# Three more w_down pairs with a second row unit by seven products, and two small kinds of buffers moved to the 2 KB pool

## The chip, the cores and the metric

One core of a Trainium2 chip (trn2) runs the whole kernel. The metric is the time of one execution on the device in microseconds (us), the median of several runs.

## The reference

Two layers of a decoder trunk on 256 tokens with 2048 features, all in fp32. What matters here is the second half of a layer, the SwiGLU block, whose last product is the one that the change touches:

```
for l in range(DEPTH):
    ...                                   # norm, projections, attention, spatial gating, merge
    x = x + merged @ w_out[l]
    h2 = rms_norm(x, ffn_norm[l])
    x = x + (jax.nn.silu(h2 @ w_gate[l]) * (h2 @ w_up[l])) @ w_down[l]
```

w_gate and w_up are 2048 x 5632, w_down is 5632 x 2048.

## The kernel before

**One product.** Every weight is read once, in halves of 256 rows x 512 columns (512 KB, tile `raw`). ScalarE (ACT) rounds a half to fp32r, tile `whi` (L261); VectorE (DVE) makes what is left over, `wlo = raw - whi` (L262). The tokens lie transposed on TensorE's other side, split the same way into `uh` and `ul`. A product of one 128-token tile with a half is six matmuls of 128x128 by 128x512: for each of two blocks of 128 rows, whi by uh, wlo by uh, whi by ul (L361, L362). An ordinary entry of the list does this for both token tiles, so twelve matmuls.

**Pairs and row units.** Column chunks of 512 are taken in pairs, a and b. A row unit is two halves (512 rows) of both chunks; with two token tiles this is a 2 x 2 by 2 x 2 product of blocks, which takes eight products of six matmuls in the plain way (entries G for a, U for b) or seven by Strassen's scheme in Winograd's form (entries P1, P5, P2, P6, P7, P4, P3, one product each). The scheme wants four differences of raw halves, made in place on DVE (L246), and so seven splits by L261 and L262 in place of four; and on the token side four sums with a split of their own: `flat`, `sums`, `sh` and `sl`, made once for a unit of tokens (L520 and L506 for unit 0, L539, L546, L551 and L552 in `summed` for unit 1). Six products are the head of a pair (P3 comes later): their entries are interleaved with the last entries of the pair ahead (L198 to L216).

Every pair has one row unit by seven products. A pair marked `two` has a second one. The raw halves of that second unit lie in the pool `big` (31 slots of 4 KB a partition), those of the first in four single buffers `k11`, `k12`, `k21`, `k22` of the pool `wraw`. When P5 is done, one accumulator is evicted to a tile `kept` (L384) and another copied (L385); P6 and P7 fold theirs into `kept` (L387); the two results start the accumulators of chunk b (L390, `acc<-kept`).

**Rounds.** The hidden width is worked in rounds of 4, 4 and 3 chunks (`ROUNDS`). A round makes its chunks of w_gate and w_up (key `ffn`, one pair of a gate and an up chunk for each f), and then multiplies by its rows of w_down: two pairs of output chunks (key `hid`, j = 0 and j = 2). The first two rounds of a layer are the middle rounds of this text: their result is a part of the residual sum. ACT evicts each accumulator to a tile `part` (L963), and a DMA on GpSimd's queue (POOL) adds it to the residual in DRAM, `held_x` (L964). The last round adds to the residual on DVE.

**What sets the order.** TensorE (PE) runs in the order in which the program is written, entry by entry. `Stream.next` asks for weights seven entries ahead, splits four ahead (`W_SPLIT`; four buffers each of whi and wlo), and makes the differences six ahead (`W_SUM`). Work on tokens is put into slots by `after` and `tick`; for the token sums of unit 1, `W_HID` is 15 slots after the ffn pair of chunk 1. The order on the other engines is set by the framework's scheduler, and each engine runs its list strictly in order. A tile of a pool takes a buffer that is free; where none is, its first writer waits for the last reader of an old one. The pool `tmp` has four buffers of 2 KB a partition.

Of the kernel before, what the change touches and what calls it, by code (L numbers as in the profile page):

```python
# [11 lines left out]
ALU = mybir.AluOpType  # L12
# [27 lines left out]
WINO_END = 9, 10, 12, 13, 14, 15  # L40
W_SPLIT = 4
X_FETCH = 2
HID_TWO = (1, 2, 2), (0, 0, 0), (1, 0, 0), (0, 0, 2), (1, 0, 2), (1, 1, 2),
W_HID = 15
FFN_TWO = (1, 0), (1, 1), (1, 2), (2, 0), (2, 1), (2, 2), (1, 3), (0, 2)
W_TWO = 17
# [17 lines left out]
def hybrid_trunk(ctx: ExitStack, tc: tile.TileContext, x, mix_norm, w_in, q_norm, k_norm, sinks,  # L64
# [299 lines left out]
    def step():  # L364
        e = entries[stream.at]
        p, tag = e["plan"], e["tag"]
        units = units_at[p.key]
        w = stream.next()
        if tag in "XGU":
            ps = banks(p, "b" if tag == "U" else "a")  # L370
            todo = [(ps[t], block(units, e["h"], t)) for t in range(NT)]
        else:
            which, t, form = {"P1": ("a", 1, (0, 0)), "P2": ("a", 0, (1, 0)), "P6": ("a", 1, 1), "P7": ("a", 1, 2),
                              "P4": ("a", 1, (1, 1)), "P5": ("a", 0, 0), "P3": ("b", 0, 3)}[tag]
            todo = [(banks(p, which)[t], tuple(x[:, form] for x in units[e["unit"]][2:]) if isinstance(form, int)
                     else block(units, 2 * e["unit"] + form[0], form[1]))]
        for ps, u in todo:
            add_product(p, ps, u, w, tag in ("P4", "P7"))
        a, b = p.acc.get("a"), p.acc.get("b")
        if not e.get("done", True):  # L380
            pass
        elif tag == "P5":
            p.kept = slot([P, 2, CW], name="kept")
            nc.scalar.activation(p.kept[:, 1, :], a[0], AF.Copy)  # L384
            nc.scalar.activation(a[0], a[1], AF.Copy)  # L385
        elif tag in ("P6", "P7"):
            nc.vector.tensor_tensor(out=p.kept[:, int(tag == "P7"), :], in0=a[1], in1=p.kept[:, 1, :], op=ALU.add)  # L387
        if "then" in e:
            for t, ps in enumerate(banks(p, "b")):
                nc.scalar.activation(ps, p.kept[:, t, :], AF.Copy)  # L390
                p.opened.add(id(ps))
        p.left -= 1
        if e is getattr(p, "last_g", None):
            p.calls[0](a)
        if p.left == 0 and p.paired:
            p.calls[1](b)
        debt[0] += len(todo)
        if debt[0] >= 2:
            debt[0] -= 2
            if p.left or p.paired:  # L400
                tick()
# [549 lines left out]
    def residual(key, nxt=None, scale=1.0, store=False, first=False):  # L951

        xt = {}

        def fetched(j):
            xt[j] = slot([P, NT, CW], name="x")
            nc.gpsimd.dma_start(xt[j], x_rows(x, j) if first else held_x[j])

        def chunk(j, sums):
            if j not in xt:  # L960
                part = slot([P, NT, CW], name="part")
                for t in range(NT):
                    nc.scalar.activation(part[:, t, :], sums[t], AF.Copy)  # L963
                nc.gpsimd.dma_start(held_x[j], part, accum_op=ALU.add)  # L964
                return
            for t in range(NT):
                n = 2 if store and j == NCH - 1 else 1
                w = CW // n
                for i in range(n):
                    sl = slice(i * w, (i + 1) * w)  # L970
                    nc.vector.scalar_tensor_tensor(out=xt[j][:, t, sl], in0=sums[t][:, sl], scalar=scale,
                                                   in1=xt[j][:, t, sl], op0=ALU.mult, op1=ALU.add)
                    if store:
                        eng = nc.sync if i == 0 else nc.scalar
                        eng.dma_start(out[0, t * P:(t + 1) * P, j * CW + i * w:j * CW + (i + 1) * w], xt[j][:, t, sl])
            if nxt is not None:
                nxt.x[j] = xt[j]
                after(5, lambda: nc.gpsimd.dma_start(held_x[j], xt[j]))
                last = j == NCH - 1 and not nxt.soon
                after(1 if last else 2, lambda: nxt.unit(j, j > 1 and nxt.soon, queue=None if last or j == 1 and nxt.soon or j == WINO and not nxt.soon else nc.gpsimd,  # L980
                                                         late=-2 if last else 0))
                after(3, lambda: nxt.squares(j))
                if j == NCH - 1:
                    after(4, lambda: nxt.finish())
                    if not nxt.soon:
                        after(W_TWO, lambda: summed(nxt.units, WINO + 1, (1, 2, 4)))

        for j in range(0, NCH, 2):
            if j == 0 and (nxt is not None or store):
                for i in range(NCH):  # L990
                    after(X_FETCH + i, lambda i=i: fetched(i))
            product_pair(key, lambda sums: chunk(j, sums), lambda sums: chunk(j + 1, sums))
        return nxt
# [146 lines left out]
```

## Time and profile before

| | |
|---|---|
| median of 3 runs | 2420.99 us (2418.62 to 2423.28) |
| profiled execution | span 2416.4 us from its first to its last instruction; 4.6 us of the median lie around it |
| instructions of the execution | 31069 |
| PE matmuls | 10692, of which 10314 are products with weights |
| DVE instructions | 2409 |
| ACT instructions | 1932 |
| granted TensorE clock | 1.000 |

How to read the profile: L261 is line 261 of the kernel; `wlo<-raw,whi` is the tile written and the tiles read; `x4` counts instructions that follow each other without a gap. In a row of the timeline come the start in us from the beginning of the span, the time that it took, the engine, the line and the operation; in square brackets, how long the engine sat idle before it and who ended that. In a row by line come the number of instructions, their busy time in us, the mean of one in ns, and the idle time before them. A matmul's own duration is longer than its share of the engine, since the next one starts before it ends; so PE is read from start to start.

### The profile page before, as it was taken

To read this page: it belongs to the slowest core of one execution; us is meant where nothing else is said; L and a number is where in the kernel's file an instruction comes from. 1 tells how busy PE (TensorE), PEld (TensorE's weight loads), DVE (VectorE), ACT (ScalarE), POOL (GpSimd) and SP (SyncE) were. 2 spreads that over 40 slices of the span, in tenths; PEclk is the share of its full clock that TensorE was granted. 3 is DMA by queue.
4 is the path that set the end of the run, shared out by engine and by line. 5 is a ranking of instruction groups with operands and counts; after the bars stand their busy time and mean duration, and the time that the engine had idled before them with its cause. 6 is when DMAs were issued, how large, how long until landed. Compare 5 with 4: busy or idle time off the path is not lost.

```text
span 2416.4 us, 31069 instructions
## 1 busy us (share of the span) xinstructions
PE 2405.1 (100%) x10692; PEld 1970.7 (82%) x10692; DVE 2092.0 (87%) x2409; ACT 1532.4 (63%) x1932; POOL 303.4 (13%) x557
## 2 busy tenths in 40 slices
PE   9999999999999999999999999999999999999999
PEld 7877888888888888888888778888888888888887
DVE  7779787898999998799887897878889989998998
ACT  6477555576666675666665775555676666666665
POOL 1100001132110111001301000011311101110010
PEclk9999999999999999999999999999999999999999
DMA  8755678687677757776957557776867786677773
GB/s 287 233 167 164 178 204 251 221 264 239 191 238 228 239 179 223 245 225 178 293 177 260 174 160 197 215 223 227 269 219 232 213 258 204 199 231 229 235 223 138
DMA packets 285070, 527.16 MB, mean 218 GB/s; under 512 B 28208, under 2 KB 40080, under 8 KB 284912
## 3 DMA queue, kind: packets, MB, share of 16 engines
q1 hardware_dynamic: 263056, 486.36, 63.6%
q0 software_dynamic: 21536, 38.56, 6.2%
q8 instruction: 83, 1.36, 0.2%
q14 instruction: 75, 0.61, 0.1%
q10 hardware_dynamic: 320, 0.27, 0.0%
HBM read 483.66 MB, written 16.78 MB: 207 GB/s over the span
## 4 chain that ended last, share of the span: by engine, by line
PE 88%; DVE 4%; DMA 4%; issue 1%; ACT 1%; SPq 1%; POOL 0%; DVEq 0%; ACTq 0%
PE acc L361 58%; PE acc L362 29%; DVE wlo L262 2%; DMA raw<-in_w_up_dram 2%; DMA raw<-in_w_in_dram 1%; DMA tt<-box 1%; ACT whi L261 1%; DVE raw L246 1%; SPq L437 1%; PE psc L807 1%; PE po L859 0%; PE psg L942 0%; PE ppt L844 0%; PE pt L474 0%; POOL tt L437 0%
## 5 line engine op out<-in xcount | busy, mean ns | idle before, releaser
L261 ACT ACTIVATE whi<-raw 128x1024 fp32r<-128x1024 f32 (+1 forms) x1116 | 1166.6, 1058 | 786.3 <-PE acc L362 440.0
L262 DVE TENSOR_TENSOR wlo<-raw,whi 128x1024 fp32r<-128x1024 f32 (+1 forms) x1117 | 1343.5, 1216 | 269.3 <-ACT whi L261 255.3
L361 PE MATMUL acc<-whi,uh 128*128 128x512 f32 x2854 | 1116.7, 391 | 1.4 <-ACT uh L460 1.4
L361 PE MATMUL acc<-wlo,uh 128*128 128x512 f32 x2854 | 1113.3, 390 | 2.1 <-DVE wlo L262 1.3
L362 PE MATMUL acc<-whi,ul 128*128 128x512 f32 x2854 | 1112.1, 390 | 0.6 <-DVE ul L465 0.6
L361 PEld LDWEIGHTS acc<-wlo,uh 128*128 128x128 f32 x2854 | 536.0, 188 | 118.5 <-DVE wlo L262 6.6
L361 PEld LDWEIGHTS acc<-whi,uh 128*128 128x128 f32 x2854 | 535.9, 188 | 117.8 <-issue 4.9
L362 PEld LDWEIGHTS acc<-whi,ul 128*128 128x128 f32 x2854 | 535.9, 188 | 112.8 <-DVE ul L465 1.5
L437 POOL DMA_DIRECT2D tt<-box x464 | 228.0, 499 | 1202.6 <-DVE box L431 339.7
L246 DVE TENSOR_TENSOR raw<-raw,raw 128x1024 f32<-128x1024 f32 x292 | 355.5, 1218 | 5.2 <-DMA raw<-in_w_up_dram 2.9
L361 PE MATMUL acc<-wlo,sh 128*128 128x512 f32 x584 | 228.1, 391 | 2.0 <-DVE wlo L262 2.0
L361 PE MATMUL acc<-whi,sh 128*128 128x512 f32 x584 | 228.4, 391 | 0.0
L362 PE MATMUL acc<-whi,sl 128*128 128x512 f32 x584 | 227.5, 390 | 0.0
L361 PEld LDWEIGHTS acc<-wlo,sh 128*128 128x128 f32 x584 | 109.7, 188 | 26.3 <-DVE wlo L262 4.1
L361 PEld LDWEIGHTS acc<-whi,sh 128*128 128x128 f32 x584 | 109.7, 188 | 25.1 <-issue 2.3
L362 PEld LDWEIGHTS acc<-whi,sl 128*128 128x128 f32 x584 | 109.6, 188 | 22.7
L387 DVE TENSOR_TENSOR kept<-acc,kept 128x512 f32<-128x512 f32 x102 | 69.6, 682 | 9.3 <-PE acc L362 9.3
L390 ACT ACTIVATE acc<-kept 128x512 f32<-128x512 f32 x102 | 59.7, 588 | 2.3 <-DVE kept L387 1.0
L964 POOL DMA_DIRECT2D held_x<-part x16 | 13.9, 868 | 301.4 <-ACT part L963 301.4
L333 POOL TENSOR_TENSOR rv<-ve,neg_half 128x4 f32<-128x4 f32 x8 | 10.2, 1273 | 266.8 <-DVE ve L907 247.9
L384 ACT ACTIVATE kept<-acc 128x512 f32<-128x512 f32 x51 | 30.1, 591 | 10.8 <-PE acc L362 10.5
L829 ACT ACTIVATE pr<-pr,negm 128x128 f32<-128x128 f32 x64 | 24.9, 390 | 16.0 <-DVE negm L820 16.0
(149 smaller groups left out, 909.0 us busy)
## 6 DMA issues: line engine op xcount, KB each, us to landing
raw<-in_w_in_dram SPq DMA_DIRECT2D x239, 512.0 KB, 4.8
raw<-in_w_gate_dram SPq DMA_DIRECT2D x176, 512.0 KB, 4.6
raw<-in_w_up_dram SPq DMA_DIRECT2D x176, 512.0 KB, 5.4
raw<-in_w_down_dram SPq DMA_DIRECT2D x176, 512.0 KB, 5.3
raw<-in_w_out_dram SPq DMA_DIRECT2D x64, 512.0 KB, 6.9
raw<-in_w_attn_branch_dram SPq DMA_DIRECT2D x64, 256.0 KB, 7.0
raw<-in_w_sgu_branch_dram SPq DMA_DIRECT2D x32, 512.0 KB, 5.8
tt<-box POOLq DMA_DIRECT2D x464, 32.0 KB, 4.7
```

What stands on the lines that cost most here:

```text
L246: self.last = nc.vector.tensor_tensor(out=self.raws[d], in0=self.raws[x], in1=self.raws[y], op=ALU.subtract)
L261: self.high = nc.scalar.activation(hi[:, i, :], raw[:, i, :], AF.Copy)
L262: self.last = nc.vector.tensor_tensor(out=lo[:, i, :], in0=raw[:, i, :], in1=hi[:, i, :].bitcast(F32), op=ALU.subtract)
L361: nc.tensor.matmul(ps, a, part[:, kk, :], start=first and kk + n == 0, stop=False, skip_group_check=True)
L362: nc.tensor.matmul(ps, b, hi[:, kk, :], start=False, stop=kk == 1, skip_group_check=True)
L384: nc.scalar.activation(p.kept[:, 1, :], a[0], AF.Copy)
L387: nc.vector.tensor_tensor(out=p.kept[:, int(tag == "P7"), :], in0=a[1], in1=p.kept[:, 1, :], op=ALU.add)
L390: nc.scalar.activation(ps, p.kept[:, t, :], AF.Copy)
L437: q.dma_start(dst[j * B:(j + 1) * B, i], box[i * B:(i + 1) * B, j])
L807: nc.tensor.matmul(pscore[:, i, :nk], self.qT[pair // 4][j * HD:(j + 1) * HD, pair % 4, t * P:(t + 1) * P], self.kT[j * HD:(j + 1) * HD, : ...
L829: self.exps = nc.scalar.activation(pr4[:, h, :], pr4[:, h, :], AF.Exp, bias=nm_[:, h:h + 1], accum_out=den[:, h:h + 1])
L964: nc.gpsimd.dma_start(held_x[j], part, accum_op=ALU.add)
```

## The change

It does three things.

- `HID_TWO` lists the w_down pairs that are `two`, as (layer, round, j). It gets three more: (0, 1, 0), (0, 1, 2) and (1, 1, 0). Before, round 0 of both layers and (1, 1, 2), (1, 2, 2) had it. Now all w_down pairs of the middle rounds have it. Since round 1 of layer 0 had none, its `summed` for the token sums of unit 1 is new as well.
- `kept` is two tiles of 2 KB in the pool `tmp` in place of one of 4 KB in `big`, but for the pairs of the key `in`.
- `part` is two tiles of 2 KB in `tmp` in place of one of 4 KB in `big`, and each is added to `held_x` by a DMA of its own, 256 KB in place of 512 KB.

```diff
-HID_TWO = (1, 2, 2), (0, 0, 0), (1, 0, 0), (0, 0, 2), (1, 0, 2), (1, 1, 2),
+HID_TWO = (1, 2, 2), (0, 0, 0), (1, 0, 0), (0, 0, 2), (1, 0, 2), (1, 1, 2), (0, 1, 0), (0, 1, 2), (1, 1, 0),
...
         elif tag == "P5":
-            p.kept = slot([P, 2, CW], name="kept")
-            nc.scalar.activation(p.kept[:, 1, :], a[0], AF.Copy)
+            if p.key[0] == "in":
+                whole = slot([P, 2, CW], name="kept")
+                p.kept = [whole[:, i, :] for i in range(2)]
+            else:
+                p.kept = [temp(name="kept") for _ in range(2)]
+            nc.scalar.activation(p.kept[1], a[0], AF.Copy)
             nc.scalar.activation(a[0], a[1], AF.Copy)
         elif tag in ("P6", "P7"):
-            nc.vector.tensor_tensor(out=p.kept[:, int(tag == "P7"), :], in0=a[1], in1=p.kept[:, 1, :], op=ALU.add)
+            nc.vector.tensor_tensor(out=p.kept[int(tag == "P7")], in0=a[1], in1=p.kept[1], op=ALU.add)
         if "then" in e:
             for t, ps in enumerate(banks(p, "b")):
-                nc.scalar.activation(ps, p.kept[:, t, :], AF.Copy)
+                nc.scalar.activation(ps, p.kept[t], AF.Copy)
...
             if j not in xt:
-                part = slot([P, NT, CW], name="part")
                 for t in range(NT):
-                    nc.scalar.activation(part[:, t, :], sums[t], AF.Copy)
-                nc.gpsimd.dma_start(held_x[j], part, accum_op=ALU.add)
+                    part = temp(name="part")
+                    nc.scalar.activation(part, sums[t], AF.Copy)
+                    nc.gpsimd.dma_start(held_x[j][:, t, :], part, accum_op=ALU.add)
                 return
```

In the changed kernel the lines from L384 on stand four lower (L388 is the old L384, L967 the old L963, L550 the old L546).

**DVE, head of the pair (0, 1, 0).** Before, in the last entries of the ffn pair f = 3 of round 1 in layer 0, one difference (L246) stands between every two or three splits (L262):

```order
L262 TENSOR_TENSOR wlo_8152<-raw_7798,whi_8151 128x1024
L262 TENSOR_TENSOR wlo_8174<-raw_8102,whi_8173 128x1024
L246 TENSOR_TENSOR raw_8102<-raw_8104,raw_8102 128x1024
L262 TENSOR_TENSOR wlo_8197<-raw_8116,whi_8196 128x1024
L262 TENSOR_TENSOR wlo_8207<-raw_8102,whi_8206 128x1024
L262 TENSOR_TENSOR wlo_8217<-raw_8171,whi_8216 128x1024
L246 TENSOR_TENSOR raw_8102<-raw_8194,raw_8102 128x1024
L262 TENSOR_TENSOR wlo_8232<-raw_8190,whi_8231 128x1024
```

Now, at the same place, with the token sums of `summed` (L550, L556) among them:

```order
L262 TENSOR_TENSOR wlo_8191<-raw_8118,whi_8190 128x1024
L246 TENSOR_TENSOR raw_8072<-raw_8074,raw_8072 128x1024
L550 TENSOR_TENSOR sums_8116<-sums_8116,flat_8114 128x256
L262 TENSOR_TENSOR wlo_8212<-raw_7782,whi_8211 128x1024
L246 TENSOR_TENSOR raw_8092<-raw_8094,raw_8092 128x1024
L550 TENSOR_TENSOR sums_8116<-flat_8114,sums_8116 128x256
L262 TENSOR_TENSOR wlo_8231<-raw_8072,whi_8230 128x1024
L262 TENSOR_TENSOR wlo_8241<-raw_8092,whi_8240 128x1024
L262 TENSOR_TENSOR wlo_8257<-raw_7819,whi_8256 128x1024
L246 TENSOR_TENSOR raw_8072<-raw_8149,raw_8072 128x1024
L556 TENSOR_TENSOR sl_8225<-sums_8116,sh_8224 128x1024
L262 TENSOR_TENSOR wlo_8268<-raw_8228,whi_8267 128x1024
```

Between the first and the last row there are now four splits, three differences and three instructions of `summed`, where there were four splits and two differences.

**ACT, end of the pair (0, 0, 0).** Before, ACT evicts the two token tiles of chunk a (the first two rows), splits four weights, and evicts chunk b:

```order
L963 ACTIVATE part_6655<-acc_6105 128x512
L963 ACTIVATE part_6655<-acc_6106 128x512
L261 ACTIVATE whi_6661<-raw_6610 128x1024
L261 ACTIVATE whi_6674<-raw_6418 128x1024
L261 ACTIVATE whi_6689<-raw_6442 128x1024
L261 ACTIVATE whi_6709<-raw_6659 128x1024
L963 ACTIVATE part_6725<-acc_6438 128x512
L390 ACTIVATE acc_6792<-kept_6536 128x512
L963 ACTIVATE part_6725<-acc_6439 128x512
L261 ACTIVATE whi_6731<-raw_6672 128x1024
```

Now the four evictions write four tiles, and two tiles `kept` of the next pair (6545 and 6546) are live:

```order
L967 ACTIVATE part_6665<-acc_6113 128x512
L967 ACTIVATE part_6668<-acc_6114 128x512
L261 ACTIVATE whi_6673<-raw_6620 128x1024
L261 ACTIVATE whi_6686<-raw_6427 128x1024
L261 ACTIVATE whi_6701<-raw_6451 128x1024
L261 ACTIVATE whi_6721<-raw_6671 128x1024
L967 ACTIVATE part_6737<-acc_6447 128x512
L967 ACTIVATE part_6740<-acc_6448 128x512
L261 ACTIVATE whi_6745<-raw_6684 128x1024
L394 ACTIVATE acc_6806<-kept_6545 128x512
```

The pool has four buffers, two hold `kept`, so part_6737 takes the buffer of part_6665 and part_6740 that of part_6668: each waits until the DMA that adds the old tile to `held_x` has landed. The split after them (whi_6745, before whi_6731) is behind both. The same order stands at the end of (0, 1, 0), (1, 0, 0) and (1, 1, 0).

## The prediction

> **What bounds the kernel now.** I read the page first, then who PE waited for, then PE's timeline.
>
> ```profile
> span 2416.4 us, 31069 instructions
> PE 2405.1 (100%) x10692; PEld 1970.7 (82%) x10692; DVE 2092.0 (87%) x2409; ACT 1532.4 (63%) x1932; POOL 303.4 (13%) x557
> ```
>
> ```profile
> engine line waited for: us in total, times, longest us
> PE acc L361 <- DVE wlo L262: 3.3, 5, 1.3
> PE acc L361 <- ACT uh L460: 1.4, 1, 1.4
> ```
>
> PE is busy for all of the span, and the waits that the profile shows add up to a few us. So time goes where matmuls go, at PE's own step from start to start. In the last entries of (0, 1, 2), where nothing waits, these are the first and the last of 26 matmuls:
>
> ```profile
> 999.95 0.39 PE L361 MATMUL acc<-whi,sh 128*128 128x512 f32 x1
> ...
> 1005.62 0.39 PE L361 MATMUL acc<-wlo,uh 128*128 128x512 f32 x1
> ```
>
> 25 steps in 5.67 us are 0.2268 us each. The 0.39 is latency and counts nothing. The next engine is DVE, and by stage it is closer than its 87%. The windows hold f = 0 to 3 of round 1 in layer 0 (757 to 928), its two w_down pairs (928 to 1004), and the first three chunks of the next round:
>
> ```profile
> core 0: us, PE busy (x) PEld busy (x) DVE busy (x) ACT busy (x) POOL busy (x), PEclk, DMA share, GB/s
> 757.00:928.00 171.00, 170.46 (x749) 139.90 (x748) 159.85 (x153) 111.70 (x126) 22.64 (x45) 1.00 0.69 214
> 928.00:1004.00 76.00, 76.00 (x336) 62.77 (x335) 58.06 (x56) 46.23 (x53) 8.27 (x16) 1.00 0.76 231
> 1004.00:1135.00 131.00, 131.00 (x578) 108.05 (x577) 118.91 (x113) 84.47 (x95) 13.51 (x26) 1.00 0.71 216
> ```
>
> DVE is busy for 159.85 of 171 us where all pairs are `two`, and for 58.06 of 76 in the w_down pairs that the change makes `two`: the 18 us free there are what it spends. In the first window PE has already stood still for DVE, in the head of f = 3:
>
> ```profile
> 890.97 0.39 PE L361 MATMUL acc<-whi,uh 128*128 128x512 f32 x1
> 891.50 0.50 PE L361 MATMUL acc<-wlo,uh 128*128 128x512 f32 x1
> ...
> 894.13 0.39 PE L361 MATMUL acc<-whi,sh 128*128 128x512 f32 x1
> 894.91 0.50 PE L361 MATMUL acc<-wlo,sh 128*128 128x512 f32 x1 [0.39 <-DVE wlo L262]
> ```
>
> The steps are 0.53 and 0.78 in place of 0.23. At 894.91, the first product of P6, DVE's lead over PE is zero. That is the point from which I add up.
>
> **The gain.** A row unit by seven products has one product less, six matmuls. Three units are 18 matmuls: 18 x 0.2268 = 4.08 us, or 0.17%. Nothing else on PE goes. The 0.2% that a measurement of this kernel can tell from no change is 4.84 us, more than the whole gain. The Trainium skill, page "TensorE: Matmul & The Clock Gate", section "Back-to-back issue gap", gives 131 ns for one of a stream of 512-column matmuls; by that the gain would be 2.4 us and the sum below 2422.5. This trace disagrees with 226.8 ns where nothing waits.
>
> **What DVE gets.** A unit adds four differences and three splits on DVE, and three splits on ACT. At full rate DVE takes these steps:
>
> ```profile
> 870.27 1.22 DVE L262 TENSOR_TENSOR wlo<-raw,whi 128x1024 fp32r<-128x1024 f32 x1
> 871.41 0.74 DVE L1080 SCALAR_TENSOR_TENSOR hid<-acc,rstd,hid 128x512 f32<-128x512 f32 x1
> 872.07 1.21 DVE L262 TENSOR_TENSOR wlo<-raw,whi 128x1024 fp32r<-128x1024 f32 x1
> ...
> 875.00 0.70 DVE L431 STREAM_TRANSPOSE box<-hid 128x512 f32<-128x512 f32 x1
> 875.63 2.32 DVE L262 TENSOR_TENSOR wlo<-raw,whi 128x1024 fp32r<-128x1024 f32 x2
> ...
> 879.81 1.22 DVE L246 TENSOR_TENSOR raw<-raw,raw 128x1024 f32<-128x1024 f32 x1
> 880.94 1.22 DVE L506 TENSOR_TENSOR ul<-flat,uh 128x1024 fp32r<-128x1024 f32 x1
> ```
>
> ```profile
> 887.29 0.42 DVE L520 TENSOR_TENSOR sums<-flat 128x256 f32<-128x256 f32 x1
> 887.63 0.42 DVE L520 TENSOR_TENSOR sums<-flat,sums 128x256 f32<-128x256 f32 x1
> ```
>
> ```profile
> L387 DVE TENSOR_TENSOR kept<-acc,kept 128x512 f32<-128x512 f32 x102 | 69.6, 682 | 9.3 <-PE acc L362 9.3
> L457 DVE TENSOR_TENSOR ul<-tt,uh 128x512 fp32r<-128x512 f32 x42 | 27.8, 684 | 1.0 <-ACT uh L456 1.0
> ```
>
> So a pass over 128x1024 costs 1.135 (1.14 and 1.13), L1080 0.66, L431 0.63, one of the token sums 0.34, and L387 and L457, which I take to overlap as the others do by some 0.08, 0.60. A unit is 7 x 1.135 = 7.9 us of DVE. Three are 24 us, and `summed` in layer 0 adds 2 x 1.135 + 4 x 0.34 = 3.6.
>
> On average that fits: 58.06 + 15.9 + 3.6 = 77.6 us of busy time (about 73 of steps) in the 73.3 us that the two pairs of layer 0 will take. But it isn't spread evenly. From the second product of P6 in f = 3, with lead zero, to the same product of the w_down pair there are 22 entries in the changed order. For PE they are 180 matmuls, 40.8 us. For DVE they are 22 splits, 8 differences and 2 passes of `summed` (32 x 1.135 = 36.3), four token sums (1.4), two each of L1080, L431, L387 and L457 (1.3 + 1.3 + 1.2 + 1.2): 42.7 us. DVE is short by 1.85 us, and with no lead to draw on, PE waits for all of it. In the kernel before, the same 22 entries hold 192 matmuls, 43.5 us, against 22 splits, 6 differences and the same eight small ones, 36.8 us: 6.7 to spare, which is why nothing is seen there. In layer 1 `summed` is there already (3.6 of the 6.7), and the changed order is the same row for row. I take 2 x 1.85 = +3.70 us. After it, the w_down pairs have no L1080 and one transpose less, and the lead grows back. The bounds: 0, if the lead at 894.91 is larger than the row shows or the small passes overlap more; 2 x 3.5, if lumps within the stretch (two differences between two splits, where an entry is worth only 1.36 us) cost as much again.
>
> ACT's three splits lie in a stage in which it is busy for 46.23 of 76 us: nothing, bounded by nothing lost while DVE is the later one.
>
> **Weights.** No byte more is loaded. But a head of two units loads the new `k22` behind the last split of the old one, and where a w_down pair (j = 2) is followed by an ffn pair this is late for DVE:
>
> ```profile
> DVE raw L246 <- DMA raw<-in_w_up_dram: 2.9, 5, 0.9
> ```
>
> ```profile
> 2217.03 0.39 PE L361 MATMUL acc<-whi,uh 128*128 128x512 f32 x1
> 2217.48 0.50 PE L361 MATMUL acc<-wlo,uh 128*128 128x512 f32 x1
> ```
>
> That is 0.22 us at the end of (1, 1, 2), and more while PE restarts. (0, 1, 2) gets the same transition: +0.25, between 0 and 1.
>
> **The 2 KB pool.** `kept` comes free in time: its waits are on transfers a pair back. The evictions of chunk b at the end of a j = 0 pair do get a new wait, four times: each for the landing of the DMA that took its buffer's old tile.
>
> ```profile
> 740.21 0.58 ACT L963 ACTIVATE part<-acc 128x512 f32<-128x512 f32 x1
> 741.35 0.60 ACT L963 ACTIVATE part<-acc 128x512 f32<-128x512 f32 x1 [0.56 <-PE acc L362]
> ...
> 742.25 0.92 POOL L964 DMA_DIRECT2D held_x<-part  x1 [25.56 <-ACT part L963]
> ...
> 748.15 0.60 ACT L963 ACTIVATE part<-acc 128x512 f32<-128x512 f32 x1 [0.25 <-PE acc L362]
> ...
> 749.51 0.60 ACT L963 ACTIVATE part<-acc 128x512 f32<-128x512 f32 x1
> 750.00 1.05 ACT L261 ACTIVATE whi<-raw 128x1024 fp32r<-128x1024 f32 x1
> ```
>
> ```profile
> DMA to landing us min/median/max: 5.2/8.0/9.9
> raw<-in_w_attn_branch_dram SPq DMA_DIRECT2D x64, 256.0 KB, 7.0
> tt<-box POOLq DMA_DIRECT2D x464, 32.0 KB, 4.7
> ```
>
> The first line is of `held_x<-part`, 512 KB. The halves can start at about 741.0 and 742.25, and their buffers are wanted at 748.15 and 749.51: 7.1 us for either. The nearest row for 256 KB says 7.0, the small DMA of the same queue 4.7, the whole part up to 9.9. I take 7.0: no wait. At 9.9 it would be 2.7 us on ACT, and what is queued behind it is the split at 750.00. The Trainium skill, "DMA: Bandwidth & Descriptors", section "Anatomy of one DMA", puts a GpSimd DMA at 2.0 us and its bytes at 436 GB/s, so 2.6 us for a half, an estimate by which this wait never comes; the 8.0 measured for the whole is far above its 3.2, so the row decides. GpSimd issues 16 DMAs more and is busy for 13% of the span: nothing.
>
> **Sum.** -4.08 + 3.70 + 0.25 + 0 = -0.13 us: a span of 2416.3 after 2416.4. The median of the runs is 4.6 above the span, so 2420.99 becomes 2420.9.
>
> **Rivals.** *DVE keeps up.* The lead is not zero where I start, or the order catches up. For it: in the head of (0, 0, 0), where `summed` lies too, nothing stands still. Against: the pair ahead of that one is not `two`. Then -4.08 + 0.25 remain: 2417.2.
>
> *The accumulating DMA is waited for.* If the queue runs the two halves one behind the other, the first at the median of the whole (741.0 + 8.0 = 749.0) and the second 5.2, the shortest, later, the second buffer comes free at 754.2, 4.7 us after it is wanted. The split behind it then starts at 754.7 and not at 750.00. What hides part of that is DVE's lead there:
>
> ```profile
> 751.09 1.23 DVE L262 TENSOR_TENSOR wlo<-raw,whi 128x1024 fp32r<-128x1024 f32 x1 [1.79 <-ACT whi L261]
> ```
>
> ```profile
> 754.97 0.39 PE L361 MATMUL acc<-wlo,uh 128*128 128x512 f32 x1
> ```
>
> That `wlo` was ready at 752.3, 2.7 us before PE came to it; in round 1 the sum above, carried on for twelve entries, leaves 1.9. So PE would lose 4.7 - 2.7 = 2.0 us and 2.8 us, twice each: +9.6, 2430.5, slower than before. It decides from the point where a half lands later than 7.1 us plus that lead after its issue. Against it: a whole part lands in 8.0, so its two halves together should not take 13.
>
> *The changed order of the lists and the looser slots in `big` shift other waits* by a us or two either way: 2419 to 2424.
>
> **Chances.** The forecast has 0.55, DVE keeping up 0.20, the DMA wait 0.15, the last 0.10. Faster by over 4.84 us needs luck of the runs (they lie 4.66 apart) on top of the second case: 0.08. Slower by over 4.84 is two thirds of the third, and a bad end of the first: 0.14. The rest, 0.78, is no change. The range goes from the second case, 2417.0, to the first with its DVE bound and some of the DMA wait, 2426.0.
>
> **What would show it.** PE has 10674 matmuls. In the timeline of f = 3 and the pair after it, steps over 0.23 us before a `wlo` matmul of P5, P6, adding up to some 1.9 us in each layer beyond those at 891 and 894. The evictions of chunk b of j = 0 start some 8 us after those of chunk a. I am wrong on DVE if PE's steps stay even there, and on the pool if ACT is seen waiting for `held_x<-part`.

## The result, and the profile after

The changed kernel takes 2432.87 us (median of 4 runs, 2431.32 to 2434.34), the kernel before 2420.52 us on the same chip (4 runs, 2418.62 to 2423.28). The ratio is 1.0052, with a 95% interval of 1.0038 to 1.0067: slower by 12.3 us, where I had said no change. The profiled executions stand 16.2 us apart in span (2432.6 after 2416.4), some 4 us more than the medians.

From the page of the kernel after, the line of the engines; there are 10674 matmuls, as said:

```profile
PE 2408.4 (99%) x10674; PEld 1967.3 (81%) x10674; DVE 2116.8 (87%) x2436; ACT 1541.3 (63%) x1942; POOL 319.1 (13%) x573
```

Who PE waits for in the kernel after (us in total, times, longest):

```profile
PE acc L361 <- DVE wlo L262: 8.2, 16, 1.1
PE acc L362 <- DVE sl L556: 7.1, 2, 3.5
```

The first line was 3.3 us in 5 waits before. The second is new, and no step of the prediction speaks of it. Here is its place in layer 0, the timeline of the kernel after (start, duration, engine, line, operation, and in brackets the idle time before it):

```profile
932.17 0.40 PE L361 MATMUL acc<-wlo,sh 128*128 128x512 f32 x1
933.69 1.23 DVE L246 TENSOR_TENSOR raw<-raw,raw 128x1024 f32<-128x1024 f32 x1 [1.24 <-DMA raw<-in_w_down_dram]
934.83 1.22 DVE L556 TENSOR_TENSOR sl<-sums,sh 128x1024 fp32r<-128x1024 f32 x1
936.10 0.67 PE L362 MATMUL acc<-whi,sl 128*128 128x512 f32 x1 [3.54 <-DVE sl L556]
...
939.12 0.63 PE L361 MATMUL acc<-whi,sh 128*128 128x512 f32 x1
939.55 0.46 PE L361 MATMUL acc<-wlo,sh 128*128 128x512 f32 x1
```

PE has come to the first product that uses the token sums of unit 1 (entry P5). `sh` is there, `sl` isn't: on DVE it stands behind a difference that a later entry needs, and that one waits 1.24 us for its weights. PE stands still from 932.17 to 936.10, and then its matmuls follow each other in 0.43 us, not 0.2268. The windows say why; the third figure from the right is the granted clock:

```profile
937.00:938.00 1.00, 1.00 (x4) 0.81 (x3) 1.00 (x2) 0.00 (x0) 0.00 (x0) 0.50 0.00 0
...
940.00:942.00 2.00, 2.00 (x11) 1.61 (x10) 1.71 (x2) 1.65 (x3) 0.00 (x0) 1.00 1.02 384
```

After the standstill the clock is at half for some 3.4 us. Standstill and slow matmuls come to 3.7 + 1.7 = 5.4 us, and layer 1 has the same at 2143.85.

The other thing that the prediction ruled out is seen too. On ACT, at the end of (0, 0, 0), the evictions of chunk b wait for the landing of the halves of chunk a, whose two DMAs are the row of POOL:

```profile
740.47 0.57 ACT L967 ACTIVATE part<-acc 128x512 f32<-128x512 f32 x1
741.27 0.60 ACT L967 ACTIVATE part<-acc 128x512 f32<-128x512 f32 x1 [0.23 <-PE acc L362]
741.34 1.81 POOL L968 DMA_DIRECT2D held_x<-part  x2 [23.59 <-ACT part L967]
...
748.87 0.60 ACT L967 ACTIVATE part<-acc 128x512 f32<-128x512 f32 x1 [1.05 <-DMA held_x<-part]
751.16 0.60 ACT L967 ACTIVATE part<-acc 128x512 f32<-128x512 f32 x1 [1.69 <-DMA held_x<-part]
751.65 1.05 ACT L261 ACTIVATE whi<-raw 128x1024 fp32r<-128x1024 f32 x1
```

Both DMAs are issued within 1.81 us, and ACT gets their buffers at 748.87 and 751.16, 2.3 us apart: the second half lands behind the first. From the rows on the tile `part`:

```profile
ACT part L967: 6.6, 5
DMA to landing us min/median/max: 3.6/7.1/9.1
```

Five such waits, 6.6 us on ACT.

**A table by place.** For each pair I took the time from its first matmul to the next pair's first, and subtracted the matmuls that run in that time at 0.2268 us each. For (0, 1, 0) of the kernel after: 922.8 to 970.3, less 180 x 0.2268, is 6.7 us; before: 927.7 to 970.0, less 186 x 0.2268, is 0.1. "Head" is f = 3 of round 1 and the pair j = 0 behind it, in both layers. "Behind" is the pair j = 2 and the first ffn pair of the next round, in both layers. The kernels are those of the next section.

| kernel | median, us | ratio to before, 95% | head | behind | rest |
|---|---|---|---|---|---|
| before | 2418.1 to 2420.5 | | 2.8 | 0.4 | 62.2 |
| after | 2432.87 | 1.0038 to 1.0067 | 16.1 | 4.2 | 65.8 |
| e3_table_only | 2428.97 | 1.0031 to 1.0057 | 15.5 | 5.4 | 60.4 |
| e2_pool_only | 2425.22 | 1.0016 to 1.0036 | 2.9 | 4.4 | 67.3 |
| e1_sums_early | 2431.55 | 1.0039 to 1.0064 | 9.7 | 9.8 | 64.0 |
| e7_sums_earlier | 2429.25 | 1.0032 to 1.0058 | 9.8 | 8.2 | 66.2 |
| e5_early_part_big | 2423.93 | 1.0011 to 1.0029 | 9.8 | 2.6 | 61.5 |
| e12_table_sums_early | 2426.84 | 1.0021 to 1.0048 | 10.4 | 5.3 | 61.9 |
| e13_no_sums | 2419.91 | 0.9999 to 1.0017 | 6.0 | 5.6 | 62.4 |
| e14_sums_on_gpsimd | 2425.91 | 1.0019 to 1.0044 | 11.4 | 4.6 | 62.5 |
| e18_f3_one_unit | 2419.61 | 0.9991 to 1.0009 | 3.9 | -0.1 | 63.5 |
| e19_late3 | 2415.42 | 0.9974 to 0.9992 | -0.1 | -0.1 | 63.6 |

In the profile of e2, 2.8 us of the rest lie in the program's first pair, which the change doesn't touch; in those of e7, e12 and e14 some 1.5 do. Each set of runs has its own before, so kernels of different sets are compared by their distances to it.

The span of after is 16.2 us longer: -4.1 for 18 matmuls, +13.3 in the head, +3.8 behind it, +3.6 in the rest, and -0.4 of rounding and of matmuls outside the pairs.

### The profile page after: what moved, and what is told of

Read it like the earlier page. It is cut to its first block, busy times and chain, and to the rows that moved or that the text cites. A ratio compares the mean times of both kernels' runs of the same rounds, so it can differ in the third digit from the quotient of the medians.

```text
span 2432.6 us, 31147 instructions
## 1 busy us (share of the span) xinstructions
PE 2408.4 (99%) x10674; PEld 1967.3 (81%) x10674; DVE 2116.8 (87%) x2436; ACT 1541.3 (63%) x1942; POOL 319.1 (13%) x573
## 3 DMA queue, kind: packets, MB, share of 16 engines
q8 instruction: 83, 1.36, 0.2%
## 4 chain that ended last, share of the span: by engine, by line
PE 76%; DVE 9%; DMA 7%; issue 5%; ACT 2%; POOL 1%; SPq 0%; DVEq 0%; ACTq 0%; POOLq 0%
PE acc L361 50%; PE acc L362 25%; DVE wlo L262 5%; DMA raw<-in_w_up_dram 2%; DMA raw<-in_w_in_dram 2%; DVE raw L246 2%; ACT whi L261 1%; DMA raw<-in_w_down_dram 1%; DMA held_x<-part 1%; PE psc L811 1%; PE po L863 0%; DVE box L435 0%; POOL tt L441 0%; DMA tt<-box 0%; DMA wsraw<-in_w_spatial_dram 0%
## 5 line engine op out<-in xcount | busy, mean ns | idle before, releaser
L262 DVE TENSOR_TENSOR wlo<-raw,whi 128x1024 fp32r<-128x1024 f32 (+1 forms) x1126 | 1354.6, 1219 | 256.0 <-ACT whi L261 242.5
L361 PE MATMUL acc<-whi,uh 128*128 128x512 f32 x2824 | 1104.6, 391 | 1.5 <-ACT uh L464 1.1
L361 PE MATMUL acc<-wlo,uh 128*128 128x512 f32 x2824 | 1101.6, 390 | 3.2 <-DVE wlo L262 2.9
L362 PE MATMUL acc<-whi,ul 128*128 128x512 f32 x2824 | 1099.8, 389 | 1.3 <-DVE ul L469 0.6
L246 DVE TENSOR_TENSOR raw<-raw,raw 128x1024 f32<-128x1024 f32 x304 | 371.1, 1221 | 9.9 <-DMA raw<-in_w_down_dram 5.4
L362 PE MATMUL acc<-whi,sl 128*128 128x512 f32 x608 | 238.4, 392 | 7.1 <-DVE sl L556 7.1
L361 PE MATMUL acc<-wlo,sh 128*128 128x512 f32 x608 | 239.4, 394 | 5.3 <-DVE wlo L262 5.3
L361 PE MATMUL acc<-whi,sh 128*128 128x512 f32 x608 | 239.3, 394 | 0.4 <-ACT sh L555 0.3
L968 POOL DMA_DIRECT2D held_x<-part x32 | 27.8, 930 | 270.9 <-ACT part L967 270.9
L388 ACT ACTIVATE kept<-acc 128x512 f32<-128x512 f32 x51 | 30.3, 595 | 26.7 <-PE acc L362 26.3
```

The lines of the kernel that those rows point to most:

```text
L246: self.last = nc.vector.tensor_tensor(out=self.raws[d], in0=self.raws[x], in1=self.raws[y], op=ALU.subtract)
L262: self.last = nc.vector.tensor_tensor(out=lo[:, i, :], in0=raw[:, i, :], in1=hi[:, i, :].bitcast(F32), op=ALU.subtract)
L361: nc.tensor.matmul(ps, a, part[:, kk, :], start=first and kk + n == 0, stop=False, skip_group_check=True)
L362: nc.tensor.matmul(ps, b, hi[:, kk, :], start=False, stop=kk == 1, skip_group_check=True)
L388: nc.scalar.activation(p.kept[1], a[0], AF.Copy)
L968: nc.gpsimd.dma_start(held_x[j][:, t, :], part, accum_op=ALU.add)
```

## The experiments

Three theories at first. A: `sl` comes late, and that is all. B: DVE is short at the head, as forecast, but by more. C: the 2 KB pool's buffers are waited for.

**One half of the change at a time.** e3_table_only is the kernel before with the new `HID_TWO`; e2_pool_only is the changed kernel with the old one:

```diff
-HID_TWO = (1, 2, 2), (0, 0, 0), (1, 0, 0), (0, 0, 2), (1, 0, 2), (1, 1, 2), (0, 1, 0), (0, 1, 2), (1, 1, 0),
+HID_TWO = (1, 2, 2), (0, 0, 0), (1, 0, 0), (0, 0, 2), (1, 0, 2), (1, 1, 2),
```

> The kernel before with the three new pairs in the table, and kept and part left as 4 KB tiles in the large pool. Theories A and B: the wait for sl (A) or the missing DVE time (B) is all there: 2429 to 2433 us, with the two waits for sl of about 3.5 us in its profile under A. Theory C: no loss, 2416 to 2418 us. If the large pool is too tight, loads of the second unit's halves come later, which would show as waits of DVE's differences or of ACT's splits for raw.

> The kernel before with kept and part in the 2 KB pool, and its own table of w_down pairs (no new row units by seven products). Theory C: this alone makes the kernel slower, by 5 us or more. Theories A and B: within 3 us of the kernel before (2420.5); what is seen are waits of ACT for the landing of the accumulating DMA, of 0.5 to 2 us at the end of a j = 0 pair that is two, three times, hidden but for some tenths.

Before is 2418.09 us on that chip. The table alone costs 10.9 us, the pool alone 7.1: both halves slow the kernel, and together (12.3) they cost less than their sum. Part of the pool's price hides behind the standstill for `sl`, as e1 and e5 show below. In e2 the pool's way to PE can be followed. ACT, at the end of (1, 1, 0):

```profile
2201.78 0.60 ACT L967 ACTIVATE part<-acc 128x512 f32<-128x512 f32 x1 [0.84 <-DMA held_x<-part]
...
2204.49 0.60 ACT L967 ACTIVATE part<-acc 128x512 f32<-128x512 f32 x1 [1.48 <-DMA held_x<-part]
2204.99 1.05 ACT L261 ACTIVATE whi<-raw 128x1024 fp32r<-128x1024 f32 x1
```

The split at 2204.99 is late, so DVE's `wlo` is, so the buffer that it frees is. The timeline of e2 goes on with SP's load of a later weight, DVE's wait for it, and PE's:

```profile
2206.07 1.23 DVE L262 TENSOR_TENSOR wlo<-raw,whi 128x1024 fp32r<-128x1024 f32 x1 [3.74 <-ACT whi L261]
2213.34 0.37 SPq L235 DMA_DIRECT2D raw<-in_w_up_dram  x1
2222.00 1.23 DVE L246 TENSOR_TENSOR raw<-raw,raw 128x1024 f32<-128x1024 f32 x1 [3.49 <-DMA raw<-in_w_up_dram]
2224.42 0.71 PE L361 MATMUL acc<-wlo,uh 128*128 128x512 f32 x1 [2.65 <-DVE wlo L262]
```

The stall comes 20 us after its cause, at another pair, and with the half clock behind it costs some 4 us in this profile. A part of it is the load itself: it lands 8.7 us after its issue (2213.34 to 2222.00), where the kernel before has 6.4 at this place (2208.69 to 2215.06).

**The token sums one step earlier, under the whole change.** e1 makes them one step earlier, as in the diff; e7 takes the operand itself two steps earlier (`late` 2 in place of 4), and the sums at `W_HID - 3`:

```diff
-                after(W_HID if f1 < NF else W_HID - 7, lambda: summed(hT, c, (1, 2, 4)))
+                if f0 == 4:
+                    after(W_HID - 1, lambda: summed(hT, c, (1, 2, 3)))
+                else:
+                    after(W_HID if f1 < NF else W_HID - 7, lambda: summed(hT, c, (1, 2, 4)))
```

> The changed kernel, but in round 1 of each layer the token sums of unit 1 start one slot earlier and their split follows one slot sooner, so that on DVE the rest sl of that split stands behind the weight split of the product that first needs it and no longer behind the fourth entry after it and its difference. Theory A (a late operand: most of the loss is PE waiting for sl, and a clock at half speed after that standstill): the two waits for sl of 3.5 us shrink to under 1.5 us each, PE's granted clock stays at 1.00 behind them, and the time falls from 2432.9 to 2420 to 2424 us. Theory B (DVE overload, my forecast: the stretch holds more DVE work than PE time): PE then waits for wlo there instead, by about 1.85 us in each layer, 2423 to 2426 us. Theory C (the loss is the new buffer waits of the 2 KB pool): no change, 2432.9.

> The changed kernel, but in round 1 of each layer the transposed tokens of chunk 1 are split two slots earlier and the token sums of unit 1 start three slots earlier, so that sl stands on DVE ahead of the weight split of the product that needs it. Theory A: no wait for sl at all, clock 1.00, about 13 us less than the changed kernel, 2419 to 2422 us. Theory B: the same work is moved into the head of f = 3, where DVE is already late, and PE waits for wlo there, 1.85 to 3.5 us more in each layer: 2423 to 2427 us. Theory C: 2432.9.

The wait for `sl` is gone in both, and with it 6.4 us of the head. But the ratio to before is 1.0052 in e1, as in the kernel after, and 1.0045 in e7, inside that kernel's interval. So A holds for the place and fails for the price. The heads still lose 9.7 us (2.8 before), now in waits for `wlo`, and "behind" grew from 4.2 to 9.8. There the pool's waits take the place of the standstill: in e1 ACT waits seven times for the landing of a half, 9.9 us, where the kernel after has five and 6.6. One of them, at the end of (0, 1, 0), and DVE's and PE's waits that follow at the first ffn pair of the next round:

```profile
1004.10 0.60 ACT L967 ACTIVATE part<-acc 128x512 f32<-128x512 f32 x1 [2.03 <-DMA held_x<-part]
...
1022.01 1.23 DVE L246 TENSOR_TENSOR raw<-raw,raw 128x1024 f32<-128x1024 f32 x1 [1.61 <-DMA raw<-in_w_up_dram]
1024.38 0.49 PE L361 MATMUL acc<-whi,sh 128*128 128x512 f32 x1 [1.03 <-ACT whi L261]
```

e5, at the end of this section, has `part` out of the pool, and 2.6 us behind in place of 9.8.

**What in the pool costs.** On the kernel before, e8 moves only `part`, e9 only `kept`, and e10 only cuts the DMA in two, with the tile left in `big`:

```diff
-                nc.gpsimd.dma_start(held_x[j], part, accum_op=ALU.add)
+                    nc.gpsimd.dma_start(held_x[j][:, t, :], part[:, t, :], accum_op=ALU.add)
```

> The kernel before, old table, with the evicted residual parts alone in the 2 KB pool; the kept sums stay in the 4 KB pool. The two moves together measured some 7 us over before. Theory C (buffers): the pool has four buffers, two held by the kept sums and two by the parts of chunk a, so that the parts of chunk b wait on ScalarE for the landing of chunk a's halves; with the kept sums out of the pool four buffers are free and that wait is gone: within 1.5 us of before (2417 to 2420), no wait of ScalarE for an accumulating DMA. Theory D (halves): twice as many accumulating DMAs, of 256 KB, cost by themselves: 4 to 7 us over before (2422 to 2425), with the wait gone all the same. Theory E (kept): the cost belongs to the kept sums' new place: 2417 to 2420, as in C, and the next kernel tells the two apart.

> The kernel before, old table, with the kept sums alone in the 2 KB pool; the evicted parts stay one 4 KB tile with one accumulating DMA of 512 KB. Theory C: no part waits for a 2 KB buffer, since none uses one: within 1.5 us of before (2417 to 2420). Theory D: the same, since no DMA is cut. Theory E: 4 to 7 us over before (2422 to 2425), with the steps of TensorE in the hid pairs, where the kept sums are.

> The kernel before, old table and old pools; only the accumulating DMA of a chunk is cut into two of 256 KB, each issued behind its own eviction. Theory C: no buffer is waited for: within 1.5 us of before (2417 to 2420). Theory D: 4 to 7 us over before (2422 to 2425). Theory E: as before.

e8 takes 2417.77 us (ratio 0.9991 to 1.0009), e9 2420.25 (0.9993 to 1.0011), e10 2419.18 (0.9989 to 1.0007), before 2418.93. None costs anything that can be told; together they cost 7. C holds: with two of four buffers held by `kept`, the parts of chunk b find none free. In e8 the rows on `part` have no wait for its own DMA, though the halves land as late as in the kernel after:

```profile
who waited for it (us, times):
  POOL held_x L964: 284.6, 29
...
DMA to landing us min/median/max: 4.0/7.0/9.0
```

**One pair alone.** e11 is the kernel before with (0, 1, 2) added to the list, and nothing else.

> The kernel before, old pools, with one of the three new pairs alone: layer 0, middle round, chunks c and d, which ran 0.8 to 0.9 us over its pitch less than before in two profiles with the new table (row 35 of the pairs). 6 matmuls less at 0.2268 us is 1.36 us. My forecast's sum: 2418.1 less 1.36, plus at most 0.3 for a weight that comes late: 2416.7 to 2417.0. Theory B (VectorE): the token sums of unit 1 are still made in this round of layer 0, since they are made where either pair of the round is listed, and they load VectorE behind f=3 of the middle round as with both pairs: then 3 to 4 us of steps there, but less, as no pair at the head needs them at once, 2418 to 2421.

(The pair that this text means is (0, 1, 2); the row numbered 35 in it belongs to the next round.) It takes 2446.34 us, 27 more than before, and the pair itself runs at its pitch. The time is lost in layer 1, where the list is as before. In e11, f = 3 of round 1 there (ACT and PE):

```profile
2111.60 0.57 ACT L384 ACTIVATE kept<-acc 128x512 f32<-128x512 f32 x1
2112.08 1.25 ACT L1076 ACTIVATE hid<-acc,rstd 128x512 f32<-128x512 f32 x2
2113.22 1.15 ACT L456 ACTIVATE uh<-tt 128x512 fp32r<-128x512 f32 x2
2114.25 0.60 ACT L385 ACTIVATE acc<-acc 128x512 f32<-128x512 f32 x1
2114.91 0.80 PE L361 MATMUL acc<-whi,sh 128*128 128x512 f32 x1 [5.53 <-ACT acc L385]
```

In the kernel before, L385 follows L384 at once (2091.32 after 2090.69). The steps of work on tokens are counted in pairs of products: a pair by seven products in one unit has an odd number of single ones, a pair with two units an even one. One more such pair shifts all later steps by half. e15 counts the second P3 of the new pair twice:

```diff
-        debt[0] += len(todo)
+        debt[0] += len(todo) + (tag == "P3" and e["done"] and plans.index(p) in (30,))
```

> The third pair alone with old pools measured 2446.34, 27 us over before, with steps in layer 1 where the table is as before, TensorE waiting for ScalarE's L385. Theory F (the count of the steps): a pair by seven products in one unit has 7 single products, in two units 14; the handlers' steps are counted by two products (debt, L404), so one more such pair moves every later handler by half a step, and in layer 1 two activations of hid and two of uh stand ahead of L385. Here the second P3 of this pair counts twice, so that all later steps are as in before; nothing else differs. Theory F: 2416.5 to 2418.5. Theory B alone: 2440 or more, as without the count.

2418.26 us where before is 2418.67, ratio 0.9986 to 1.0004: all 27 us are gone. What is left is -1.36 us for six matmuls, and a loss of 1.07 at the end of the new pair, where DVE waits for a load:

```profile
1013.90 1.22 DVE L246 TENSOR_TENSOR raw<-raw,raw 128x1024 f32<-128x1024 f32 x1 [1.57 <-DMA raw<-in_w_up_dram]
1016.32 0.50 PE L361 MATMUL acc<-wlo,uh 128*128 128x512 f32 x1 [0.79 <-DVE wlo L262]
```

This is the transition for which the prediction put +0.25. In the change of this text the count differs from that of the kernel before only between (0, 1, 0) and (0, 1, 2) and behind (1, 1, 0); whether that costs there wasn't run by itself.

**How short DVE is.** Three kernels with the new table and the old pools (before: 2418.67). e12 has the early sums of e1; e13 leaves the token sums out; e14 makes them on GpSimd:

```diff
+                    after(W_HID, lambda: hT.__setitem__(c, (*hT[c], *(u.rearrange("p k (t q) -> p k t q", q=P) for u in hT[c]))))
...
+                    after(W_HID - 1, lambda: summed(hT, c, (1, 2, 3), nc.gpsimd))
```

> The new table with the old pools (that measured 2428.97), and the token sums of unit 1 in the middle round one step earlier, so that the low halves sl stand ahead of the split of entry 417 on VectorE. Theory A (the late operand): the two standstills of 3.4 to 3.6 us for sl and the half clock behind them go, some 11 us, and nothing takes their place: 2416 to 2419. Theory B (VectorE is short by more than my 1.85 us per layer, and a standstill of TensorE only gave it time to catch up): the steps before the wlo matmuls come in its stead, as with the new pools, where the same edit brought 1.3 us: 2426 to 2429.

> The new table with the old pools, and the token sums of unit 1 in the middle round left out: the products that use sums take the plain halves uh and ul of the unit instead, so the numbers computed there are others. This takes 1.14 + 4 x 0.31 + 1.14 = 3.5 us per layer from VectorE (flat, four sums, sl), 1.04 us from ScalarE and the wait for sl; all other work stays. Theory A: as the kernel with early sums, 2414 to 2418, since only the wait mattered. Theory B: with a shortage of about 4 us per layer at the head, 3.5 us less leave at most 1 us per layer there, and the late weights behind it get fewer too: 2417 to 2421, some 7 to 11 us below the kernel with early sums. If both kernels are within 2 us of each other and over 2425, neither holds, and the seven products themselves (their eight raw differences, or the ring of raw buffers) are the cost.

> The new table with the old pools, the token sums of unit 1 in the middle round one step earlier and made by GpSimd in place of VectorE (flat, four sums, sl); the results are the same. Theory B: VectorE gets 3.5 us per layer back, as in the kernel that leaves the sums out, if GpSimd's chain of flat, sums and sl is done by the use of sh and sl: 2417 to 2422. If GpSimd takes twice VectorE's time for each pass (no row of this case shows one), its chain of some 7 us and ScalarE's 1.04 us still fit between the steps, or sl comes late again by some us: up to 2430. Theory A: 2416 to 2419, if sl is in time.

e12 keeps 8.2 us over before without any wait for `sl`: -4.1 for the matmuls, +7.6 in the heads and +4.9 behind. e13, with 3.5 us per layer less for DVE, is 6.9 us faster than e12; the profiles show 4.4 of it in the heads and nothing behind. So B holds, in the heads. In e12, DVE's window for the head of layer 0 (time, PE, PEld, DVE busy):

```profile
881.00:970.00 89.00, 86.02 (x372) 68.70 (x371) 87.06 (x90) 57.22 (x64) 17.71 (x37) 1.00 0.62 195
```

It is busy for 87.06 of 89 us (78.58 before). What is left are two waits, in e12's timeline of DVE:

```profile
937.22 1.23 DVE L246 TENSOR_TENSOR raw<-raw,raw 128x1024 f32<-128x1024 f32 x1 [1.33 <-DMA raw<-in_w_down_dram]
...
942.46 0.69 DVE L387 TENSOR_TENSOR kept<-acc,kept 128x512 f32<-128x512 f32 x1 [0.53 <-PE acc L362]
```

From 894.20 up to the first of them DVE has no pause. The load that it waits for is one of a row of four, whose first SP issues as soon as a split of DVE has freed its buffer (e12's timelines of DVE and SP):

```profile
926.73 1.22 DVE L262 TENSOR_TENSOR wlo<-raw,whi 128x1024 fp32r<-128x1024 f32 x1
927.97 8.32 SPq L235 DMA_DIRECT2D raw<-in_w_down_dram  x4
```

The split ends at 927.95, and the load lands at 937.1. A DVE that is late gets such loads late; how much of the 1.33 us is due to that was not run by itself.

e14 brought 0.9 us of the 7. GpSimd was in time, but slow, and DVE with it:

```profile
910.44 3.21 POOL L539 TENSOR_TENSOR flat<-uh,ul 128x1024 f32<-128x1024 f32 x1 [20.55 <-DVE ul L457]
...
910.19 1.22 DVE L262 TENSOR_TENSOR wlo<-raw,whi 128x1024 fp32r<-128x1024 f32 x1
911.32 3.42 DVE L246 TENSOR_TENSOR raw<-raw,raw 128x1024 f32<-128x1024 f32 x1
```

**What is lost behind the heads** is mostly another wait. 3.1 of e12's 5.3 us are two steps of PE that wait for ACT's L385, at P6 of (0, 1, 2) and of (1, 1, 2). The first, in e12's timelines of ACT and PE:

```profile
978.45 0.58 ACT L384 ACTIVATE kept<-acc 128x512 f32<-128x512 f32 x1
979.97 2.01 ACT L261 ACTIVATE whi<-raw 128x1024 fp32r<-128x1024 f32 x2 [0.94 <-DVE raw L246]
981.88 0.58 ACT L385 ACTIVATE acc<-acc 128x512 f32<-128x512 f32 x1
982.51 0.50 PE L361 MATMUL acc<-whi,sh 128*128 128x512 f32 x1 [1.29 <-ACT acc L385]
```

Two splits stand between L384 and L385, and the first waits for a difference of DVE. The kernel before has one split there, and none in layer 1. e13 has this wait too, although DVE has less to do. Another 1.9 us are late loads, as in e15.

**Where the shortage sits.** e18 is e12 with the pair f = 3 of round 1 back to one unit, so that DVE comes to the new pair with a lead. It also has e15's line, for f = 3 and the three new pairs: its steps are counted as in the kernel before, and those of e12 are off by half a step behind the new pairs.

```diff
-FFN_TWO = (1, 0), (1, 1), (1, 2), (2, 0), (2, 1), (2, 2), (1, 3), (0, 2)
+FFN_TWO = (1, 0), (1, 1), (1, 2), (2, 0), (2, 1), (2, 2), (0, 2)
```

> The kernel with the new table, the old pools and the early sums (2426.84), with the pair f=3 of the middle round by seven products in one unit in place of two, in both layers, and the count of the steps kept as there. It has 12 matmuls more (2.72 us) and 6 raw differences less per layer on VectorE ahead of the new pairs, 4 of 1.13 us for the second unit's own plus those that come with the six products it no longer has. Theory B (VectorE comes out of f=3 without a lead, and the new pair adds its shortage there): with the lead kept, the rows f=3 to the second new pair run within 1 us of their pitch, and the time is 2418.5 less 6 x 0.2268 less f=3's own 1.3 us per layer, 2414.5 to 2418. If the shortage lies in the new pairs themselves, wherever the lead stands: 2424 to 2430.

2419.61 us (before 2419.55): by the distances to before it is 8.1 below e12, with 12 matmuls more. The heads fall from 10.4 to 3.9, "behind" from 5.3 to nothing. What the heads lose in e12 is lost ahead of the second P3 of the first new pair, and up to there the count is the same in both. So this part is the lead's: the shortage belongs to the two heads in a row, not to the new pairs alone. But e12's waits for L385 lie where the count differs too, so there e18 doesn't tell the lead from the count. One wait is left, in e18:

```profile
935.49 1.14 ACT L456 ACTIVATE uh<-tt 128x512 fp32r<-128x512 f32 x2
936.53 0.58 ACT L384 ACTIVATE kept<-acc 128x512 f32<-128x512 f32 x1
937.24 1.06 ACT L261 ACTIVATE whi<-raw 128x1024 fp32r<-128x1024 f32 x1
938.20 0.58 ACT L385 ACTIVATE acc<-acc 128x512 f32<-128x512 f32 x1
938.83 0.50 PE L361 MATMUL acc<-whi,sh 128*128 128x512 f32 x1 [1.68 <-ACT acc L385]
```

e19 takes the operands of f = 2 one step later (`late` 3 in place of 2 where `f0 == 4`), so that L385 follows L384 ahead of them.

> The kernel with f=3 by one unit (2419.61), and the transposed operands of f=2 in the middle round taken one step later, so that on ScalarE L385 follows L384 of the new pair directly, ahead of one split and of the two uh. There TensorE stood 1.7 us per layer for L385 with VectorE 4.6 us ahead. If that wait is all that is left of the new pairs' price: 2419.6 less 2 x 1.84 is 2415.9, 2415 to 2417, under before by 3 to 4 us. If VectorE's lead is used up in its place, by the operands that now come later: 2418 to 2421.

2415.42 us (11 runs, 2411.93 to 2418.92) where before is 2419.80: ratio 0.9983, 0.9974 to 0.9992. It has 6 matmuls fewer than the kernel before (1.36 us) and none of the 2.8 us that f = 3 lost there. It beats both kernels, and it is e3 with four edits, in the old pools.

**One tenant taken out of the pool under the change.** e5 is e1 with `part` back in `big`, one DMA of 512 KB; `kept` stays in the pool.

> The changed kernel with the early sums (2431.55), and the residual parts back in the 4 KB pool with one accumulating DMA; the kept sums stay in the 2 KB pool. Theory C (the two tenants of the 2 KB pool block each other): no wait of ScalarE for an accumulating DMA, and the time falls to that of the new table with the old pools and early sums, 2426.8: 2425 to 2428. If the pool's cost was only another place of VectorE's shortage: 2430 to 2432, as with the parts in the pool.

2423.93 us, ratio 1.0020 where e1 had 1.0052: 7.7 us by the ratios, from this place alone. So the pool's price stands beside DVE's, and is paid under the new table too once `sl` is in time. e5 is also some 3 us below e12, whose `kept` lies in `big`; by the intervals these two overlap.

## Why the prediction was wrong

**The gain** was right. In e15 six matmuls fewer and the late load make -1.36 + 1.07 = -0.3 us, and -0.4 was measured; in e19 -1.36 and the 2.8 of f = 3 make -4.2, and -4.4 was measured, each with an interval of some 2 us to either side.

**DVE's shortage** was the right mechanism at the right place, of the wrong size. "DVE is short by 1.85 us" summed what DVE has to do and took it to do that without a pause. e12 measures it without the late `sl`: 10.4 - 2.8 = 7.6 us in the heads, 3.8 per layer. The difference is DVE's own waits there, 1.33 + 0.53 = 1.86 us, beside the 1.85. An engine without a lead can get its weights late too, since its own passes free the buffers that the loads wait for. The upper bound, 7.0 us for both layers, comes near, but its reason was another, lumps of work.

**What the step left out: when `sl` is due.** The sum counts the pass of `summed` among 32 passes, as time, and not as an operand. PE needs it at P5; in DVE's list it stood behind a difference and a split for later entries, in rows that the part on the change prints. It cost 2 x 5.4 us where it stands. What it costs net is less and not settled: without it the ratio stayed at 1.0052 with the new pool (e1), and went from 1.0044 to 1.0034 with the old ones (e3, e12), within their intervals.

**Weights at +0.25, and nothing else behind the heads,** failed too. The load at the end of (0, 1, 2) costs 1.07 us in e15. e12 loses 4.9 us more behind the heads than the kernel before: 1.8 by late loads and other waits for `wlo`, and 3.1 in waits for L385, for which the sum has no term. Whether DVE's lateness, ACT's order or the count of the steps makes these 3.1 stays open. "The lead grows back" itself holds: at 1003 of e12 DVE waits for ACT again.

**The pool at nothing** failed. The step set 7.0 us of landing against 7.1 until the buffer is wanted (7.3 for the second half, by its own rows), and took a margin of 0.1 us for none to pay. The halves land in up to 9.1, and a wait of 1 to 2 us on ACT moves splits, `wlo`, buffers and loads after it, to a stall of 3 us at another pair. That was the rival with 0.15. Its reason, one half behind the other, is seen in the landings, but at 2.3 us and not at the 5.2 that it took. e8 and e10 have the same halves and pay nothing, since nobody waits for them there: it takes `kept` in two of the four buffers as well.

**The rivals**: DVE keeping up is out; shifted waits are real (e11: 27 us by half a step) but weren't priced as such. The range ended at 2426.0: it held DVE's upper bound with some of the pool's wait, and neither the losses behind the heads nor the late `sl`.

## What to carry to other kernels

Where an engine's lead is zero, sum its waits with its work, and look up for each operand that it makes when the consumer first needs it, not only what it costs. Count the live tiles of every tenant of a small pool at the moment of the tightest request; a margin below the spread of a DMA's landing (here 3.6 to 9.1 us) is a wait. A small gain by fewer matmuls is to be had where the other engines have a lead, and it can be worth taking work out of the stretch ahead to make one.

## What the runs showed of the hardware

**Half the clock after some 2.2 us.** Standstills of PE from 2.2 us (start to start of the matmuls on both sides) up were followed by half the clock in all ten cases in the middle parts of these runs (2.2 to 5.9 us); single ones up to 2.07 us were not (two in a row were, of 1.99 and 1.26 us in e1). At 2.2 us it goes either way: near the program's end one of 2.20 us was followed by half the clock in e19 and one of 2.20 us was not in e10. In e13, a standstill of 2.20 us, and soon behind it 0.43 us a matmul for 3 us:

```profile
977.79 0.39 PE L362 MATMUL acc<-whi,ul 128*128 128x512 f32 x1
979.99 0.50 PE L361 MATMUL acc<-whi,sh 128*128 128x512 f32 x1 [1.82 <-ACT acc L385]
...
980.97 0.63 PE L361 MATMUL acc<-whi,sh 128*128 128x512 f32 x1
981.40 0.63 PE L361 MATMUL acc<-wlo,sh 128*128 128x512 f32 x1
```

The wait at 938.83 of e18, 2.07 us, left the clock at 1.00. The Trainium skill, page "TensorE: Matmul & The Clock Gate", section "What's actually happening", has the clock fall after an idle window of about 3.4 us and rise after a busy one; the time at half agrees, the idle time that it takes is shorter here.

**GpSimd passes stop DVE.** A pass over 128x1024 takes 3.21 us on GpSimd where DVE takes 1.22, and DVE's difference that began 0.88 us into it ended only 1.09 us after it, 3.42 us long. Layer 1 of e14 shows the same pair of times. The Trainium skill, page "SBUF — State Buffer", section "SBUF: two separate sides", says that GpSimd and a DVE operation with two inputs from SBUF lock a shared port for a whole instruction; this trace agrees.
